# Placing each weight chunk at its own offset in its tile: a decoder layer on one core

## The chip, the cores and the metric

One Trainium2 chip, one of its cores. The metric is the device time of one execution in microseconds. The engines are TensorE (PE, its weight loads shown as PEld), VectorE (DVE), ScalarE (ACT), GpSimd (POOL) and SyncE (SP), which here only issues DMAs.

## The reference

The reference is one decoder layer on a residual stream x of 512 tokens by 1024 features in float32. An RMS norm and a projection w_in give inputs for two mixers. One is a pooling mixer with windows of 2, 4, 8 and 16 tokens, each followed by a 128 x 128 matrix. The other is a sparse attention of 8 heads with 64 features in two groups: it adds a compressed branch (blocks of 32 tokens), a selected branch and a window branch, weighted by sigmoid gates. Cut to what matters:

```
proj = rms_norm(x) @ w_in
y_pool = pooling_mixer(u) @ w_pool_out
y_nsa  = nsa_mixer(q, kv, gates) @ w_nsa_out
x = x + (gate_pool * y_pool + gate_nsa * y_nsa) @ w_out
gate_pre, val = split(rms_norm(x) @ w_up)          # 1024 -> 2 x 2816
x = x + (silu(causal_dwconv(gate_pre)) * val) @ w_down
```

With 512 tokens there are 8 blocks of 64 tokens to select from and up to 16 may be selected, so the kernel computes the selected and the window branch as full causal attention.

## The kernel before, in words

Activations are kept feature-major: 128 features on the partitions, 512 tokens along them, one such tile being a page of 2048 bytes per partition. `page()` takes them from one pool of PAGES buffers (L51).

Precision is bought with split operands. A float32 operand is cut into a high half in the matmul's number format (float32r) and a low half, which is the rest, and `mm3` (L390) issues three matmuls for each 128-row slice: high by high, high by low, low by high.

`weights()` (L373) brings a weight chunk. It takes three tiles of 1024 columns: wraw for the DMA from HBM, issued on SP; whi and wlo for the two halves. There are three buffers of each, used in turn. With lo="d" ScalarE writes -raw into wlo, a DMA issued on POOL adds raw to it in place, which leaves what the rounding of -raw had cut off, and ScalarE writes whi. Otherwise ScalarE writes whi and VectorE subtracts it from raw into wlo. The chunks come in this order of calls:

- 8 chunks of wa (768 columns) in `round_a`: queries and keys, tokens on the output partitions; here x is the stationary operand and the weights are moved, 512 and 256 columns at a time.
- 22 chunks of wf and 4 of wpo in `feature` and `pool_out`, the "feature stream", with lo="d": keys and values for the compression, pooling inputs and gates. From here on the weights are the stationary operand: 128 columns at a time are loaded, and 512 columns of activations are moved past them.
- 4 chunks of wno, 8 of wout, 44 of wup, 24 of wdn (16 with 1024 columns, 8 with 768): the dense stages that end the kernel.

A chunk of 1024 columns feeds 24 matmuls.

The order of the instructions is not the order in which the code calls them. All calls are recorded by a class `Plan`, with a price in us for each and with their dependencies; `run` (L212) then lists them, engine by engine, starting whatever can start first, and `emit` tries TRIES times with due times that come from the try before. On TensorE two streams are kept, the main one (attention and all later stages) and the feature stream, and they are mixed by the share done of each. A tile can only be given out when a buffer of its tag is free: the number of pages thus has a part in the order. wraw, whi and wlo are given out strictly in the order of calls (`FIFO`).

In the profile all of this has line L339, where the planner calls the engines; instructions are told apart by their tiles. mm, tr, av and sc are PSUM banks, xh and xl the halves of the normed input, oh and ol of the attention's output, mh and ml of the merged mixers, gh and gl of the input of the conv-MLP, yh and yl of its product, pp the attention's weights, qt and kt queries and keys.

Of the kernel before, what the change touches and what calls it, by code (L numbers as in the profile page):

```python
# [9 lines left out]
F32R = mybir.dt.float32r  # L10
# [5 lines left out]
P = 128  # L16
# [31 lines left out]
    CST[_n] = (_o, _o + _w)  # L48
    _o += _w
NCST = _o  # L50
PAGES = 54  # L51
TRIES = 8
RESERVE = 3
BASE = 5.0
# [288 lines left out]
def hybrid_layer(ctx: ExitStack, tc: tile.TileContext, xT, pos, par, cst, poolw, w1, wa, wb, wf,  # L343
                 wpo, wno, wout, wup, wdn, out):
    nc = tc.nc
    pl = Plan(nc)
    PE, ACT, DVE, POOL, SP = pl.engines
    sb = ctx.enter_context(tc.tile_pool(name="sb", bufs=1))
# [4 lines left out]
    def f32(ap):  # L353
        return ap.bitcast(F32)

    def page(name, shape=(P, T), dt=F32):
        return pl.tile(sb, shape, dt, name, "pg", PAGES)

# [6 lines left out]
    def split(dst_hi, dst_lo, src, scale=None):  # L365
# [3 lines left out]
        else:  # L369
            ACT.activation(dst_hi, src, AF.Copy, scale=scale)  # L370
            DVE.scalar_tensor_tensor(dst_lo, src, scale, f32(dst_hi), op0=ALU.mult, op1=ALU.subtract)

    def weights(ap, width, lo="d"):  # L373
        raw = pl.tile(sb, (P, 1024), F32, "wraw", "wraw", 3)
        hi = pl.tile(sb, (P, 1024), F32R, "whi", "whi", 3)
        low = pl.tile(sb, (P, 1024), F32R, "wlo", "wlo", 3)
        SP.dma_start(raw[:, :width], ap)
        if lo == "d":
            ACT.activation(low[:, :width], raw[:, :width], AF.Copy, scale=-1.0)
            POOL.dma_start(low[:, :width], raw[:, :width], accum_op=ALU.add)  # L380
            ACT.activation(hi[:, :width], raw[:, :width], AF.Copy)
        else:
            ACT.activation(hi[:, :width], raw[:, :width], AF.Copy)
            DVE.tensor_sub(low[:, :width], raw[:, :width], f32(hi[:, :width]))
        return hi, low
# [102 lines left out]
    for k in range(KD):  # L488
        if k < KD - 1:
            load_x(k + 1)  # L490
        xh[k], xl[k] = page("xh", dt=F32R), page("xl", dt=F32R)
        split(xh[k], xl[k], xr[k], mixg[:, k:k + 1])
        wak[k] = weights(wa[k], 768, "v")
        if k == 6:
            for j in range(KD):
                square_x(j)
            norm_rstd(acc, rstd, "mm")
            DVE.tensor_scalar_mul(rhalf, rstd, 0.5)
        round_a(k)
        if k == 1:  # L500
            SP.dma_start(ps_i, pos)
            SP.dma_start(cs, cst)
            SP.dma_start(pr[:, 16:], par[:, 16:])
# [47 lines left out]
    for c, (k0, k1) in enumerate(((0, 3), (3, 6), (6, 8))):  # L551
        raw = pl.tile(sb, (P, 1024), F32, "wraw", "wraw", 3)
        SP.dma_start(raw[:, :(k1 - k0) * 280], flat(wb[:, k0:k1]))
        for j in range(k1 - k0):
            home = ("pp", 10) if len(bw) < 5 else ("pt", 6)
            hi, lo = (pl.tile(sb, (P, 280), F32R, n, home[0], home[1]) for n in ("bh", "bl"))
# [88 lines left out]
    def feature(i, hi, lo):  # L645
        wh, wl = weights(flat(wf[i]), 1024)
        pt = bank("mm")
        mm3(pt, wh, wl, hi, lo, 0, KD)
        return pt
# [8 lines left out]
    with pl.on("f"):  # L658
# [50 lines left out]
        def pool_out(c):  # L709
            wh, wl = weights(wpo[c].rearrange("p a k n -> p (a k n)"), 1024)  # L710
            for f in (2 * c, 2 * c + 1):
                o = (f % 2) * 512
                pt = bank("mm")
                mm3(pt, wh[:, o:o + 512], wl[:, o:o + 512], yph, ypl, 0, 4)
                DVE.scalar_tensor_tensor(gpy[f], gpy[f], 1.0, pt, op0=ALU.add, op1=ALU.mult)
                SP.dma_start(gdr[f], gpy[f])
# [252 lines left out]
    for c in range(4):  # L969
        wh, wl = weights(wno[c].rearrange("p a k n -> p (a k n)"), 1024, "v")  # L970
        for f in (2 * c, 2 * c + 1):
# [12 lines left out]
            hi, lo = page("mh", dt=F32R), page("ml", dt=F32R)  # L984
# [11 lines left out]
    for f in range(8):  # L996
# [10 lines left out]
        hi, lo = page("gh", dt=F32R), page("gl", dt=F32R)  # L1007
# [13 lines left out]
    for f in range(KF):  # L1021
# [12 lines left out]
        if f < 8:  # L1034
            home = ("pp", 10) if f < 5 else ("pt", 6)
            hi, lo = (pl.tile(sb, (P, T), F32R, n, home[0], home[1]) for n in ("yh", "yl"))
        else:
            hi, lo = page("yh", dt=F32R), page("yl", dt=F32R)
# [112 lines left out]
```

## Time and profile before

| | |
|---|---|
| median of two runs | 717.29 us (716.8 to 717.78) |
| the profiled execution's own time | 717.68 us |
| its span, first to last instruction | 715.9 us |
| granted TensorE clock | 1.00 |
| TensorE busy | 709.5 us, 3494 instructions |
| VectorE, ScalarE, GpSimd busy | 417.7, 328.9, 31.0 us |
| moved by DMA | 90.80 MB, 127 GB/s on the mean |

In the rows of the profile "mm<-xh,whi 128\*128 128x512" is a matmul into bank mm with a stationary operand of 128 x 128 and a moving one of 128 x 512; "x176 | 73.3, 417 | 0.3" are its count, busy time in us, mean length in ns and the idle time before it. Matmuls overlap: one lasts longer than the step from its start to the start of the next, and it is the step that adds up to the span. A row of the timeline has the start in us, the length in us, the engine, the line, the operation and tiles, and a count where neighbours were merged.

### The profile page before, as it was taken

Reading aid. Unit: us, or ns where it says so; the run is one execution under the profiler, and the core shown is the slowest. Engines: PE = TensorE matmul, PEld = TensorE weight load, DVE = VectorE, ACT = ScalarE, POOL = GpSimd, SP = SyncE. Lnnn points to the kernel's source line nnn. Section 1 sums busy time; section 2 is a strip of 40 time slices with the busy share of each in tenths; the row PEclk is TensorE's granted clock in tenths of the full one; section 3 lists DMA queues with packets and bytes.
Section 4 is the critical chain, followed back from the end, with each engine's and each line's share of the span. In section 5 each row is a group of like instructions: output and inputs, shape, how many; then the busy total and the mean of one; then the engine's idle time right before and its main releaser. Section 6 shows DMA issues by size and latency. Waiting matters only on the chain.

```text
span 715.9 us, 9305 instructions
## 1 busy us (share of the span) xinstructions
PE 709.5 (99%) x3494; PEld 595.3 (83%) x3494; DVE 417.7 (58%) x874; ACT 328.9 (46%) x548; POOL 31.0 (4%) x43
## 2 busy tenths in 40 slices
PE   9999999999999999999999999999999999999997
PEld 8898888888888888888888888888888888888886
DVE  6768478878766643865576556656655663222220
ACT  8567368767677663433443343334333432121220
POOL 0001300000001000000000000000000000000000
PEclk9999999999999999999999999999999999999999
DMA  8476242654655567744322332232232333434320
GB/s 309 153 181 211 60 118 68 168 135 122 157 147 134 147 162 248 266 126 164 108 89 88 96 111 88 89 117 88 89 113 94 89 86 106 132 96 119 102 67 29
DMA packets 30573, 90.80 MB, mean 127 GB/s; under 512 B 3648, under 2 KB 3776, under 8 KB 30528
## 3 DMA queue, kind: packets, MB, share of 16 engines
q1 hardware_dynamic: 26640, 76.56, 32.5%
q0 software_dynamic: 3744, 13.63, 10.1%
q8 instruction: 27, 0.44, 0.2%
q14 instruction: 18, 0.15, 0.1%
q10 hardware_dynamic: 144, 0.01, 0.0%
HBM read 70.27 MB, written 6.29 MB: 107 GB/s over the span
## 4 chain that ended last, share of the span: by engine, by line
PE 99%; DVE 1%; issue 0%; ACT 0%; POOL 0%; ACTq 0%; POOLq 0%
PE mm L339 42%; PE tr L339 40%; PE av L339 13%; PE sc L339 3%; DVE kc L339 0%; DVE th L339 0%; DVE o L339 0%; DVE ks L339 0%; DVE qs L339 0%; ACT qs L339 0%; POOL ones L339 0%; ACTq L339 0%; ACT kt L339 0%; POOLq L1142 0%
## 5 line engine op out<-in xcount | busy, mean ns | idle before, releaser
L339 ACT ACTIVATE whi<-wraw 128x1024 fp32r<-128x1024 f32 (+1 forms) x114 | 117.2, 1028 | 213.0 <-PE tr L339 78.5
L339 DVE TENSOR_TENSOR wlo<-wraw,whi 128x1024 fp32r<-128x1024 f32 (+1 forms) x88 | 103.4, 1175 | 76.1 <-ACT whi L339 75.8
L339 PE MATMUL mm<-xh,whi 128*128 128x512 f32 x176 | 73.3, 417 | 0.3
L339 PE MATMUL mm<-xl,whi 128*128 128x512 f32 x176 | 69.0, 392 | 0.0
L339 PE MATMUL mm<-xh,wlo 128*128 128x512 f32 x176 | 69.0, 392 | 0.0
L339 PE MATMUL tr<-gh,whi 128*128 128x512 f32 x168 | 65.4, 390 | 0.0
L339 PE MATMUL tr<-gl,whi 128*128 128x512 f32 x168 | 65.4, 389 | 0.0
L339 PE MATMUL tr<-gh,wlo 128*128 128x512 f32 x168 | 65.4, 389 | 0.0
L339 PE MATMUL mm<-gh,whi 128*128 128x512 f32 x120 | 46.8, 390 | 0.0
L339 PE MATMUL mm<-gh,wlo 128*128 128x512 f32 x120 | 46.7, 389 | 0.0
L339 PE MATMUL mm<-gl,whi 128*128 128x512 f32 x120 | 46.7, 389 | 0.0
L339 PE MATMUL tr<-yh,whi 128*128 128x512 f32 x110 | 42.8, 389 | 0.0
L339 PE MATMUL tr<-yl,whi 128*128 128x512 f32 x110 | 42.8, 389 | 0.0
L339 PE MATMUL tr<-yh,wlo 128*128 128x512 f32 x110 | 42.8, 389 | 0.0
L339 PEld LDWEIGHTS mm<-xh,wlo 128*128 128x128 f32 x176 | 33.0, 188 | 7.5
L339 ACT ACTIVATE pp<-pp,asm 128x128 f32<-128x128 f32 (+3 forms) x64 | 35.3, 554 | 7.5 <-DVE asm L339 7.3
L339 PEld LDWEIGHTS mm<-xh,whi 128*128 128x128 f32 x176 | 33.2, 189 | 5.7 <-DVE th L339 1.1
L339 PEld LDWEIGHTS tr<-gl,whi 128*128 128x128 f32 x168 | 31.5, 188 | 6.5
L339 PEld LDWEIGHTS tr<-gh,whi 128*128 128x128 f32 x168 | 31.5, 188 | 6.6
L339 PEld LDWEIGHTS tr<-gh,wlo 128*128 128x128 f32 x168 | 31.5, 188 | 6.5
L339 PEld LDWEIGHTS mm<-xl,whi 128*128 128x128 f32 x176 | 33.3, 189 | 3.7
L339 ACT ACTIVATE ft<-ft 128x512 f32<-128x512 f32 x22 | 13.9, 632 | 44.1 <-DVE ft L339 44.0
(295 smaller groups left out, 1509.1 us busy)
## 6 DMA issues: line engine op xcount, KB each, us to landing
wraw<-wup SPq DMA_DIRECT2D x44, 512.0 KB, 3.3
wlo<-wraw POOLq DMA_DIRECT2D x26, 512.0 KB, 4.5
wraw<-wf SPq DMA_DIRECT2D x22, 512.0 KB, 3.4
wraw<-wdn SPq DMA_DIRECT2D x16, 512.0 KB, 3.5
wraw<-wout SPq DMA_DIRECT2D x8, 512.0 KB, 3.7
wraw<-wa SPq DMA_DIRECT2D x8, 384.0 KB, 5.2
wraw<-wdn SPq DMA_DIRECT2D x8, 384.0 KB, 3.1
xr<-xT SPq DMA_DIRECT2D x8, 256.0 KB, 6.4
```

Source lines behind the costliest of these rows:

```text
L339: getattr(self.real[o.eng], method)(*a, **kw)
```

## The change

whi and wlo become 64 columns (256 bytes) longer, and each call of `weights()` has a running number n, from 1 on. The high half of chunk n begins 4 (n mod 16) columns into its tile, which is 16n bytes modulo 256; the low half begins 4 (5n mod 16) columns into its own, 80n bytes modulo 256. All that reads or writes the halves goes by these slices. wraw stays as it is. The six tiles grow by 1536 bytes per partition together, and PAGES goes from 54 to 53, which gives up 2048.

```diff
-PAGES = 54
+PAGES = 53
...
+    shift = [0]
+
     def weights(ap, width, lo="d"):
         raw = pl.tile(sb, (P, 1024), F32, "wraw", "wraw", 3)
-        hi = pl.tile(sb, (P, 1024), F32R, "whi", "whi", 3)
-        low = pl.tile(sb, (P, 1024), F32R, "wlo", "wlo", 3)
+        n = shift[0] = shift[0] + 1
+        hi = pl.tile(sb, (P, 1088), F32R, "whi", "whi", 3)[:, n % 16 * 4:n % 16 * 4 + 1024]
+        low = pl.tile(sb, (P, 1088), F32R, "wlo", "wlo", 3)[:, n * 5 % 16 * 4:n * 5 % 16 * 4 + 1024]
         SP.dma_start(raw[:, :width], ap)
         if lo == "d":
             ACT.activation(low[:, :width], raw[:, :width], AF.Copy, scale=-1.0)
```

## The prediction

> **What bounds the kernel now.** I read the page first: the busy times, the chain and the costliest groups.
>
> ```profile
> span 715.9 us, 9305 instructions
> PE 709.5 (99%) x3494; PEld 595.3 (83%) x3494; DVE 417.7 (58%) x874; ACT 328.9 (46%) x548; POOL 31.0 (4%) x43
> ...
> PE 99%; DVE 1%; issue 0%; ACT 0%; POOL 0%; ACTq 0%; POOLq 0%
> PE mm L339 42%; PE tr L339 40%; PE av L339 13%; PE sc L339 3%; DVE kc L339 0%; DVE th L339 0%; DVE o L339 0%; DVE ks L339 0%; DVE qs L339 0%; ACT qs L339 0%; POOL ones L339 0%; ACTq L339 0%; ACT kt L339 0%; POOLq L1142 0%
> ...
> L339 ACT ACTIVATE whi<-wraw 128x1024 fp32r<-128x1024 f32 (+1 forms) x114 | 117.2, 1028 | 213.0 <-PE tr L339 78.5
> L339 DVE TENSOR_TENSOR wlo<-wraw,whi 128x1024 fp32r<-128x1024 f32 (+1 forms) x88 | 103.4, 1175 | 76.1 <-ACT whi L339 75.8
> ```
>
> TensorE is busy for 99% of the span and is 99% of the chain. The view of waits for that engine leaves it almost nothing else:
>
> ```profile
> PE mm L339 <- POOL ones L339: 1.0, 1, 1.0
> PE tr L339 <- DVE qs L339: 0.8, 1, 0.8
> PE tr L339 <- ACT qt L339: 0.2, 1, 0.2
> ```
>
> It waits 2.0 us in all. So the time is the number of matmuls times the step from one start to the next (not the 389 ns of one, since they overlap), and I went to the timeline of TensorE for that step. First the up-projection just after a few small matmuls:
>
> ```profile
> 357.39 0.40 PE L339 MATMUL mm<-gl,whi 128*128 128x512 f32 x1
> 357.62 0.40 PE L339 MATMUL mm<-gh,wlo 128*128 128x512 f32 x1
> ...
> 358.09 0.39 PE L339 MATMUL mm<-gl,whi 128*128 128x512 f32 x1
> 358.31 0.39 PE L339 MATMUL mm<-gh,wlo 128*128 128x512 f32 x1
> ...
> 359.47 0.39 PE L339 MATMUL mm<-gl,whi 128*128 128x512 f32 x1
> ...
> 359.93 0.39 PE L339 MATMUL mm<-gh,whi 128*128 128x512 f32 x1
> ...
> 362.42 0.39 PE L339 MATMUL mm<-gh,wlo 128*128 128x512 f32 x1
> ```
>
> From 357.39 to 359.47 lie nine matmuls: 2.08 / 9 = 231.1 ns each, uneven ones (358.09 to 358.31 is 0.22 us). From 359.93 to 362.42 lie eleven: 2.49 / 11 = 226.4 ns, all equal. Later it stays like that:
>
> ```profile
> 400.05 0.39 PE L339 MATMUL tr<-gh,wlo 128*128 128x512 f32 x1
> 400.27 0.39 PE L339 MATMUL tr<-gh,whi 128*128 128x512 f32 x1
> ...
> 401.86 0.39 PE L339 MATMUL tr<-gl,whi 128*128 128x512 f32 x1
> ```
>
> Eight steps in 1.81 us are 226.3 ns; I use 226.5. The stream thus has a settled step of 226.5 ns and an unsettled one of 231.1 ns, and needs about nine matmuls after a disturbance to settle. In the stage where attention and feature chunks alternate it seldom settles:
>
> ```profile
> 214.77 1.11 PE L339 MATMUL sc<-kt,qt 128*128 128x256 f32 x8
> 215.72 0.40 PE L339 MATMUL mm<-xh,whi 128*128 128x512 f32 x1
> 215.95 0.40 PE L339 MATMUL mm<-xl,whi 128*128 128x512 f32 x1
> 216.19 0.39 PE L339 MATMUL mm<-xh,wlo 128*128 128x512 f32 x1
> ...
> 217.11 0.60 PE L339 MATMUL tr<-cs,pp 128*128 128x128 f32 x4
> ```
>
> Six matmuls from 215.72 to 217.11 take 1.39 us, 231.7 ns each, and the longest step, 215.95 to 216.19, is 0.24 us. Eight 256-wide ones before them take 0.95 us, 119 ns each.
>
> **The change, part by part.** *The number of instructions.* None is added or removed: the 3434 matmuls of the program, its copies and its DMAs are the same. What changes is the address from which each weight load reads, the address to which ScalarE, VectorE and the accumulating DMA write, and, through the page count, the planner's order.
>
> *The weight loads.* In the dense stages the weights are the stationary operand: 4 chunks of wno, 8 of wout, 44 of wup and 24 shorter ones of wdn give 96 + 192 + 1056 + 528 = 1872 matmuls of 512 columns, and the 26 chunks of the feature stream 624 more, 2496 in all. Every large tile of the built kernel starts at 128 modulo 256 bytes and each 128-column slice is 512 bytes long, so every weight load and every moving read starts at the same place modulo 256. No row shows another placement; the price has to be bounded. That steps of one shape and one granted clock come out at 226.5 or 231.1 ns, by what ran just before, tells me that the reads are sensitive to their phase. A weight load lies beside the matmul ahead of it:
>
> ```profile
> L339 PEld LDWEIGHTS tr<-gh,whi 128*128 128x128 f32 x168 | 31.5, 188 | 6.6
> L339 PEld LDWEIGHTS tr<-gl,whi 128*128 128x128 f32 x168 | 31.5, 188 | 6.5
> ```
>
> At 188 ns it fits in the 226.5 ns, with 38 ns to spare, so a load that only lengthened by a few ns would cost nothing. What can cost is the step itself. Lower end of the usual kind: every chunk settles at once, 0 us. Upper end: none settles, 1872 x (231.1 - 226.5) = 1872 x 4.6 ns = 8.6 us. My value goes by the nearest row, the nine unsettled matmuls after a disturbance: each chunk now starts at another offset than the one before it, so I count nine unsettled matmuls in each of the 1872 / 24 = 78 full chunks' worth: 78 x 9 x 4.6 ns = 3.2 us. In chunks with an odd n the two halves lie 64 or 192 bytes apart, modulo 256, and the stream goes back and forth between them; that this keeps them unsettled is possible, and it is what the upper end holds. The feature stream is unsettled already (231.7 ns), so it gets nothing.
>
> *Weights as the moving operand.* In the first stage xh is stationary and whi, wlo are moved, 8 chunks x 24 matmuls 512 wide = 192. Bounded by the same 4.6 ns either way, +-0.9 us. I take 0.
>
> *ScalarE and VectorE.* The splits write and read at shifted places. A slower one is covered as long as these engines have room in the dense stage:
>
> ```profile
> 400.00:450.00 50.00, 50.00 (x222) 41.38 (x222) 29.14 (x36) 18.80 (x23) 0.00 (x0) 1.00 0.32 105
> ```
>
> Columns: TensorE, weight loads, VectorE 29.14 and ScalarE 18.80 us of 50, at a granted clock of 1.00. A chunk lasts 24 x 226.5 = 5.4 us, VectorE needs 3.2 of it, so its 1175 ns subtraction could grow by 2.2 us before it is late. I take 0, bounds 0 to 0.
>
> *The accumulating DMA.* Its destination is no longer at the same place modulo 256 for each chunk. From the view of tile wlo in the feature stage:
>
> ```profile
> L339 PE MATMUL mm<-xh,wlo x176: 387/392/417, 54.6 to 285.3; 128*128 128x512 f32 x176
> L339 POOL DMA_DIRECT2D wlo<-wraw x25: 859/862/934, 38.0 to 269.5; - x25
> ...
> DMA to landing us min/median/max: 4.5/4.5/7.2
> ```
>
> The last one is issued at 269.5 and lands at 274.0; the last matmul on its chunk starts at 285.3 and the first seven triples earlier, 7 x 0.69 = 4.9 us, so at 280.4. The least slack is 6.4 us, and the transfer may last 2.4 times as long before TensorE waits. Behind it on the POOL queue stand only the other accumulates. I take 0; what it would be without the cover is a rival.
>
> *One page fewer.* The order on TensorE moves between about the fifth and the eleventh chunk of the feature stream and is nearly the same afterwards; on SP one load of a feature chunk moves past a store of a gate and two reloads of tn swap places with gp; on POOL one accumulate moves behind two additions of kcb. TensorE can win no more than its 2.0 us of waits; a missing page could hold one chunk back, 5.4 us at most if nothing else were ready. Nearest is the present state, hardly any wait: 0, bounds -2.0 and +5.4.
>
> *Sum.* The profiled execution took 717.68 us (span 715.9 and 1.8 around it), 0.4 above the median of 717.29. 717.7 + 3.2 = 720.9, on the median 720.5.
>
> A rule of the Trainium skill speaks against this term: TensorE: Matmul & The Clock Gate, Part 2, step 1, says that TensorE reads weights and the moving operand by two independent ports, so that loading the next weights takes no bandwidth from the running matmul. By that rule the term is 0 and the sum 717.3 on the median; the trace's two steps for one shape do not fit it, but no run here varies the address.
>
> **The rivals.** *No influence of the address (not slower, not faster).* The steps differ by the mix of instructions alone and the weight loads read beside it all. For it: 38 ns of spare time after each load. Against it: 231.1 ns within one chunk, with nothing but 512-wide matmuls, settling only after nine. It gives 717.3, plus the order's -2 to +5.
>
> *Faster: the reads stop colliding.* Two 256-wide steps make 238 ns and one 512-wide 226.5; a straight line through 119 and 226.5 ns has a slope of 107.5 ns per 256 columns and 11.5 ns that do not grow with the width. If that part is a collision of weight load and moving read at equal addresses and spreading ends it, 2496 x 11.5 = 28.7 us go: 688.6. Over 2%, 14.3 us, needs 5.7 ns of it, a mean step of 220.8. Against it: no step in the quoted rows is under 0.22 us even where phases vary, and the spread goes through all offsets, so good and bad ones mix. The middle, 703, is what I would expect of it. The same page of the Trainium skill, Back-to-back issue gap, has 512 / 2.4 + 2.5 = 215.8 ns; by that figure an estimate of the most to be won is 2496 x 10.7 = 26.7 us.
>
> *Slower by over 2%: a worse beat that holds.* Halves at different offsets keep the whole dense part at the longest step seen, 0.24 us by rounded starts, so at least 235 ns: 1872 x 8.5 = 15.9 us, and 624 x (235 - 231.7) = 2.1 us in the feature stream: 735.3. It decides from a dense step of 234.1 on (14.3 / 1872 = 7.6 ns). For it: such steps occur singly. Against it: they have always been mixed with short ones.
>
> *Slower: the accumulate or a page.* The quoted row has 25 accumulates from 38.0 to 269.5, one in 9.6 us. If a transfer took three times as long, 13.5 us, each would come 3.9 us later than the one before it, and 24 x 3.9 less the slack of 6.4 is 87 us. Against it: it needs a threefold transfer. A page held back costs the 5.4 us above.
>
> **How the numbers follow.** The likeliest case, unsettled starts of chunks, has 0.30 and gives 720.5, with its own range of 717 to 726. No influence has 0.22, at 717.3. Both are within 2%: 0.52. A worse beat has 0.24, transfers and pages 0.07: slower by over 2%, 0.31. Collisions that end have 0.17. Two per cent is about what a measurement of this kernel can tell from no change. The range takes in half of the faster case and the worse beat with some of the order's loss: 702 to 740; some 0.12 lies below it and 0.07 above.
>
> **What would show it.** In the profile after: the step between 512-wide matmuls in the dense stage, chunk by chunk, since n is known for each. Nine uneven steps of about 231 ns at a chunk's start and 226.5 after them would show the term right; 226.5 throughout, no influence; steps under 0.22, the faster rival; 235 and more, the slower. Whether odd n differ from even n tells if the distance between halves matters. The landing of wlo<-wraw near 4.5 us, and TensorE waits near 2 us, would show the other terms at 0. I am wrong if TensorE is no longer 99% of the chain.

## The result, and the profile after

The changed kernel takes 728.01 us in the median of two runs (727.65 to 728.37) against 717.29: a ratio of 1.0149, 95% interval 1.0106 to 1.0193. It is 1.5% slower: less than the 2% from which the prediction counts a change, though the interval leaves no doubt of the sign. The profiled execution took 727.65 us, 9.97 more than that of before, and its span is 10.0 us longer.

From the page of the changed kernel, the span, the busy times, the chain and three of the groups:

```profile
span 725.9 us, 9304 instructions
PE 719.8 (99%) x3494; PEld 595.4 (82%) x3494; DVE 419.6 (58%) x874; ACT 328.3 (45%) x548; POOL 30.5 (4%) x43
...
PE 98%; DVE 1%; DMA 0%; ACT 0%; issue 0%
...
L339 DVE TENSOR_TENSOR wlo<-wraw,whi 128x1024 fp32r<-128x1024 f32 (+1 forms) x88 | 103.4, 1175 | 77.2 <-ACT whi L339 77.2
...
L339 PE MATMUL tr<-gh,whi 128*128 128x512 f32 x168 | 66.3, 395 | 0.0
...
L339 PEld LDWEIGHTS tr<-gh,whi 128*128 128x128 f32 x168 | 31.6, 188 | 7.2
```

TensorE has as many records and is busy for 10.3 us longer; of the other engines none changes by more than 2 us. A weight load still lasts 188 ns, VectorE's subtraction still 1175 ns. Only the matmul is longer, 395 ns where it was 389 to 390.

TensorE makes up 98% of the chain and not 99%, which the prediction named as a sign of being wrong. By lines it is 98.1% after 98.5%, and what came in is 0.4% of the first weight loads (DMA wraw<-wa), so the bound is still TensorE. Its waits in the changed kernel add up to 1.9 us, against 2.0:

```profile
PE mm L339 <- POOL ones L339: 1.0, 1, 1.0
PE mm L339 <- DVE kc L339: 0.6, 1, 0.6
PE tr L339 <- ACT xh L339: 0.3, 1, 0.3
```

Where the time comes from is shown by the first and the last matmuls of the dense stages, from the views of the tiles oh and yh. The two times after the lengths are the first and the last start in us. Before:

```profile
L339 PE MATMUL tr<-oh,whi x20: 389/389/389, 285.5 to 306.6; 128*128 128x512 f32 x20
L339 PE MATMUL tr<-yh,wlo x110: 388/389/389, 592.5 to 711.5; 128*128 128x512 f32 x110
```

After:

```profile
L339 PE MATMUL tr<-oh,whi x20: 390/397/398, 285.7 to 307.3; 128*128 128x512 f32 x20
L339 PE MATMUL tr<-yh,wlo x110: 387/394/399, 599.8 to 721.4; 128*128 128x512 f32 x110
```

Up to the dense part the two kernels differ by 0.2 us (285.5 and 285.7). The dense part takes 711.5 - 285.5 = 426.0 us before and 721.4 - 285.7 = 435.7 after: 9.7 of the 10.0 us. The mean step there, worked out from all starts in the trace except four longer steps across the small matmuls of the norm, rose from 226.70 to 231.94 ns, and 1872 x 5.24 ns = 9.8 us.

The timeline of TensorE shows how, since n is known for each chunk. These are the edges of the chunks 63, 64 and 65 of the changed kernel; each bank's 24 matmuls are one chunk:

```profile
443.46 0.39 PE L339 MATMUL mm<-gh,whi 128*128 128x512 f32 x1
...
448.99 0.39 PE L339 MATMUL tr<-gh,whi 128*128 128x512 f32 x1
...
454.43 0.39 PE L339 MATMUL av<-gh,whi 128*128 128x512 f32 x1
454.66 0.40 PE L339 MATMUL av<-gl,whi 128*128 128x512 f32 x1
...
456.99 0.39 PE L339 MATMUL av<-gh,wlo 128*128 128x512 f32 x1
```

Chunk 64, with both halves at 0, takes 5.44 us for 24 steps: 226.7 ns, settled from its first matmul. Chunk 63 (240 and 176 bytes) takes 5.53 us, 230.4 ns. In chunk 65 (16 and 80 bytes) the ten steps from 454.66 on take 2.33 us, 233 ns. What follows the first nine steps of a chunk is no shorter than the whole: 231.82 ns in the mean over the 16 values of n mod 16, against 231.94. So most chunks are not unsettled for a while and then settled; each value of n mod 16 has a mean step that comes back, within about 0.5 ns, each time the value does (chunks 48 and 49, next to the norm's small matmuls, excepted) and holds to the end of the chunk. Odd and even n do not differ: 231.9 ns each.

The accumulating DMA shows nothing; its landing in the feature stream of the changed kernel:

```profile
L339 POOL DMA_DIRECT2D wlo<-wraw x25: 859/859/899, 37.5 to 269.3; - x25
...
DMA to landing us min/median/max: 4.5/4.5/7.3
```

### The profile page after: what moved, and what is told of

The parts are those of the page before. It is cut to its first block, busy times and chain, and to the rows that moved or that the text cites. A ratio compares the mean times of both kernels' runs of the same rounds, so it can differ in the third digit from the quotient of the medians.

```text
span 725.9 us, 9304 instructions
## 1 busy us (share of the span) xinstructions
PE 719.8 (99%) x3494; PEld 595.4 (82%) x3494; DVE 419.6 (58%) x874; ACT 328.3 (45%) x548; POOL 30.5 (4%) x43
## 4 chain that ended last, share of the span: by engine, by line
PE 98%; DVE 1%; DMA 0%; ACT 0%; issue 0%
PE mm L339 41%; PE tr L339 40%; PE av L339 13%; PE sc L339 3%; DMA wraw<-wa 0%; DVE th L339 0%; DVE kc L339 0%; ACT xh L339 0%; DVE o L339 0%; DVE ks L339 0%; ACT whi L339 0%; ACT kt L339 0%; ACT ks L339 0%
## 5 line engine op out<-in xcount | busy, mean ns | idle before, releaser
L339 DVE TENSOR_TENSOR wlo<-wraw,whi 128x1024 fp32r<-128x1024 f32 (+1 forms) x88 | 103.4, 1175 | 77.2 <-ACT whi L339 77.2
L339 ACT ACTIVATE wlo<-wraw 128x1024 fp32r<-128x1024 f32 x26 | 27.5, 1059 | 15.5 <-PE mm L339 12.8
```

The costliest lines, as they stand in the source:

```text
L339: getattr(self.real[o.eng], method)(*a, **kw)
```

## The experiments

The theory (A in the texts below): the step between matmuls depends on where the weight load starts, modulo 256, relative to the moving operand, and lastingly so. Its rivals: (B) the planner's order with one page fewer costs the time; (C) only the changing of places unsettles the stream; (A2) the weights' own place counts, whatever the moving operand's is; and that ScalarE, VectorE or the DMAs bring the cost in. Runs 1, 2 and 12 are medians of 10, 4 and 10 executions, the others are one execution each. Executions of one kernel differ by up to 1.5 us (run 1: 716.35 to 717.81), so the argument goes by the dense step, worked out from the trace as above.

**1. Pages and tile length without the shift.** Edit to the changed kernel:

```diff
-        hi = pl.tile(sb, (P, 1088), F32R, "whi", "whi", 3)[:, n % 16 * 4:n % 16 * 4 + 1024]
+        hi = pl.tile(sb, (P, 1088), F32R, "whi", "whi", 3)[:, 0:0 + 1024]
...
+        low = pl.tile(sb, (P, 1088), F32R, "wlo", "wlo", 3)[:, 0:0 + 1024]
```

> Tiles of 1088 columns and 53 pages as in the changed kernel, with the planner's order of it, but every half at offset 0. Theory A (the place of the weights relative to the moving operand sets the step): the dense step is 226.7 ns again, the time 717 to 718 us. Theory B (the order with one page fewer costs the time): about 728 us, with the dense step still at 226.7 ns, since that stage has no choice of order.

Measured: 717.38 us, ratio to the kernel before 0.9992, interval 0.9982 to 1.0001; dense step 226.70 ns. Theory B falls: with the instructions in the same order as in the changed kernel the whole loss is gone.

**2. Both halves at 64 bytes, always.** As 1, with 16 in place of 0 in both lines.

> Both halves of every chunk at 64 bytes. Theory A: the chunks with both halves at 64 bytes stepped at 233.3 ns in the changed kernel, so the whole dense part does: 1872 x (233.3 - 226.7) = 12.4 us over the kernel without shift, about 730 us. Theory C (only changes from chunk to chunk and from half to half unsettle the stream, any constant place settles): 226.7 ns and 717 to 718 us.

Measured: 731.18 us, ratio 1.0185, interval 1.0168 to 1.0202; dense step 233.34 ns from the first chunk to the last. Theory C falls: nothing changes from chunk to chunk here and the stream never settles at 226.7. Its timeline has a beat of two:

```profile
400.63 0.40 PE L339 MATMUL tr<-gh,whi 128*128 128x512 f32 x1
400.86 0.39 PE L339 MATMUL tr<-gl,whi 128*128 128x512 f32 x1
401.09 0.40 PE L339 MATMUL tr<-gh,wlo 128*128 128x512 f32 x1
401.33 0.39 PE L339 MATMUL tr<-gh,whi 128*128 128x512 f32 x1
...
404.83 0.40 PE L339 MATMUL tr<-gh,whi 128*128 128x512 f32 x1
```

From 400.63 to 404.83 lie 18 matmuls in 4.20 us: 233.3 ns each, longer and shorter by turns.

**3 and 4. One offset for both halves, in lines of 16 bytes and in single columns.** As the changed kernel, with `n % 16 * 4` in both lines, and with `n % 16` in both.

> Both halves at 16n bytes modulo 256, so the two halves never differ. Theory A: a step for each of the 16 places, 226.7 ns at 0, 233.3 at 64 and 128, 229.3 at 192, others between 226.7 and 235; time 726 to 730 us. Theory C: each chunk unsettled for its first nine matmuls and 226.7 after that: 721 us.

Measured: 726.84 us; mean dense step 231.64 ns. With both halves at the same place the loss is nearly that of the change, so the distance between the halves is not what matters most. At 0 and 240 bytes, and in four of the five chunks at 16 bytes, the stream steps at 226.7 for most of a chunk, elsewhere at 229.2 (192 bytes) to 234.3 (96 bytes).

> Both halves at 4n bytes modulo 64, so single columns. Theory A says that the step depends on the place; if a line of 16 bytes is what counts, the four places within a line give one step, and 0 to 12 bytes give 226.7 ns; 16, 32 and 48 bytes give what the run with 16n shows. A step below 226.7 anywhere would make a faster kernel. Theory C: 721 us, alike for all places.

Measured: 728.32 us; mean 232.15 ns. The guess about lines of 16 bytes was wrong: at 4, 8 and 12 bytes the step is 232.3, 230.9 and 230.0 (last fifteen steps of a chunk), within 16 bytes of the place that gives 226.7.

The two runs also show that the place alone does not always fix the step. A chunk at 16 bytes follows one at 0 bytes in run 3 and one at 12 bytes in run 4. Here is one of each, from its first matmul to the first of the next chunk. Run 3:

```profile
454.19 0.39 PE L339 MATMUL av<-gh,whi 128*128 128x512 f32 x1
...
459.64 0.39 PE L339 MATMUL mm<-gh,whi 128*128 128x512 f32 x1
```

Run 4:

```profile
471.56 0.39 PE L339 MATMUL tr<-gh,whi 128*128 128x512 f32 x1
...
477.16 0.39 PE L339 MATMUL mm<-gh,whi 128*128 128x512 f32 x1
```

The 24 steps take 5.45 and 5.60 us: 227 and 233 ns at the same place. In run 3 itself, the first chunk at 16 bytes starts just after the norm's small matmuls and keeps 233.3 ns to its end, while the four later ones have 227.0. So at some places the stream can hold more than one step, and what ran before decides between them. Theory A does not say this, and theory C has that much in its favour.

**5 and 6. Moving the pages.** 5 is kernel 1 with a tile of 64 bytes allotted ahead of the pages, 6 is 5 with both halves at 192 bytes.

```diff
     ones = keep("ones", (P, P))
+    pad = keep("pad", (P, 16))
+    POOL.memset(pad, 0.0)
```

> No shift within the weight tiles, but 64 bytes of padding ahead of the pages, so that pages and weights both lie at 192 modulo 256 instead of 128. If the place relative to the moving operand counts (theory A): 226.7 ns and 717 to 718 us. If the weights' own place modulo 256 counts (A2): 233.3 ns as with both halves at 64 bytes, about 731 us.

Measured: 716.98 us; dense step 226.71 ns.

> The same padding, and both halves at 192 bytes in their tiles: the weights lie at 128 modulo 256 as in the kernel before, the pages at 192. Theory A: the place of the weights relative to the pages is 192, which stepped at 229.2 ns in the changed kernel: 1872 x 2.5 = 4.7 us, about 722 us. A2: 226.7 ns and 717 to 718 us.

Measured: 720.74 us; dense step 228.90 ns. Here the weights lie exactly where they lie, modulo 256, in the kernel before, and the step is that of 192 bytes. Both runs say that the place relative to the pages counts, and A2 falls. From 6:

```profile
400.02 0.39 PE L339 MATMUL tr<-gh,wlo 128*128 128x512 f32 x1
...
402.31 0.39 PE L339 MATMUL tr<-gh,whi 128*128 128x512 f32 x1
```

Ten steps in 2.29 us: 229 ns.

**7. Only wraw shifted.** Kernel 1 with wraw 1088 columns long and its data 64 bytes in, and 52 pages (which changes the planner's order once more).

> Only wraw is shifted, by 64 bytes, and the halves stay at 0 (52 pages, to make room): the DMA writes and ScalarE, VectorE and the accumulating DMA read at another place than before, TensorE does not. Theory A: 226.7 ns and 717 to 719 us. If the placement hurts by way of the other engines' accesses, the dense step rises as with the halves at 64 bytes, towards 731 us.

Measured: 718.15 us; dense step 226.70 ns. The accesses of the DMA, ScalarE and VectorE at the shifted place cost nothing that shows in the step.

**8. The stream by itself.** The layer is left out; sections of 96 matmuls run on fixed tiles, between two short ones, with nothing else at work:

```python
for i in range(count):
    a, b = (i // 3 % 8) * P + w(i) % 64, (i % 8) * 512 + m(i) % 64
    nc.tensor.matmul(pt[0:cols, 0:n], W[:, a:a + cols], M[:, b:b + n], start=True, stop=True)
```

> None of the layer is computed: only sections of 96 matmuls each on fixed tiles, and no other engine at work. Theory A: with weights 0, 16, 64, 128 and 192 bytes past the moving operand's place the steps are 226.7, 226.7, 233.3, 233.3 and 229.2 ns as in the layer, so that TensorE's two reads alone make them; both moved together by 64 or 192 bytes give 226.7. With a moving operand that starts 16, 32, 48, 64 or 128 bytes further on for each matmul the step may fall below 226.7, to 216 if a full round of lines is what the settled step waits for (224 to 236 otherwise). Loads of 32, 64 and 96 columns: 218, 221 and 224 ns if each line of a load costs the same, 226.7 if loads cost nothing at this place. Widths of 256, 384, 448, 480, 496: 120, 173, 200, 213 and 227 ns if the step goes in units of 13.33 ns; 113, 170, 198, 213 and 220 if it goes with the width.

Steps after the first thirty of a section, from the starts in the trace (the sections with the weights at 0, 16 and 32 bytes run together in the records; their joint stretch steps at 226.7 ns for its first two thirds and at 233.3 for the last):

| weights, moving operand at (bytes) | step, ns |
|---|---|
| 64, 0 / 128, 0 / 192, 0 | 233.4 / 232.3 / 228.9 |
| 64, 64 / 192, 192 | 226.7 / 226.7 |
| 0, 64 / 0, 192 | 228.9 / 233.3 |
| 0, further on by 16, 32, 48, 64, 128, 224, 240 each time | 230.5, 234.2, 231.6, 231.7, 230.1, 231.7, 235.0 |
| both further on by 16, 32, 64 each time | 230.4, 232.5, 228.3 |
| 0, 0 with 32, 64, 96 columns loaded | 231.6, 229.9, 230.0 |
| 0, 0 with 256, 384, 448, 480, 496 columns moved | 120.0, 173.3, 206.7, 216.7, 223.3 |

The layer's steps at 64, 128 and 192 bytes come back to within about 1 ns without any other engine, so TensorE's two reads are enough to make them. Moving operand at 64 with the weights at 0 is as good as weights at 192 with the moving operand at 0, as theory A has it. The rest of the guesses went wrong: a moving operand that walks on is never below 226.7; loads of fewer columns don't shorten the step, they lengthen it by 3 to 5 ns. Widths of 256 and 384 columns, and 512 of the settled layer, step at 120.0, 173.3 and 226.7: 53.3 ns for each 128 columns, and 13.3 ns that do not grow with them. The widths of 448, 480 and 496 lie 3 to 7 ns above that line.

**9. All 64 places.** As 8, sections of 48, the weights 0 to 252 bytes past the moving operand's place. The steps are those after the first twenty of a section.

> None of the layer is computed: 64 sections of 48 matmuls of 512 columns, with the weights 0, 4, 8 ... 252 bytes past the place of the moving operand, nothing else at work. Theory A: 226.7 ns at 0, the values of the layer at 64, 128 and 192 bytes (233.3, 233.3 and 229.0), and nothing below 226.7, so that the placement of the kernel before is already the best. If the collision of equal places were what the fixed 13.3 ns are (the faster rival), some places would step at 216 to 220.

Nothing steps below 226.67 ns. That value comes at 0, 16, 28, 120, 132 and 156 bytes; 31 places lie within 0.4 ns of 233.3, the others from 228.3 (240 bytes) to 238.0 (164 bytes). The expected 233.3, 233.3 and 229.0 at 64, 128 and 192 bytes were 233.3, 232.4 and 228.9. Most places that runs 3 and 4 also had agree with them within 1 ns; 12, 28 and 240 bytes, as well as 16, do not (233.3, 226.7 and 228.3 here; 230.0 and 234.9 in run 4 and 226.7 in run 3). The table is thus that of this order of places, each entered after the short matmuls between sections. The timeline merges each section into one row; here are the sections at 0, 4, 8, 12 and 16 bytes:

```profile
20.77 11.15 PE L372 MATMUL pt<-m,w 128*128 128x512 f32 x48
...
32.23 11.39 PE L372 MATMUL pt<-m,w 128*128 128x512 f32 x48
...
43.94 11.32 PE L372 MATMUL pt<-m,w 128*128 128x512 f32 x48
...
55.57 11.44 PE L372 MATMUL pt<-m,w 128*128 128x512 f32 x48
...
67.33 11.13 PE L372 MATMUL pt<-m,w 128*128 128x512 f32 x48
```

The second column is the section's length: 11.15 and 11.13 us at 0 and 16 bytes, 11.32 to 11.44 between.

**10 and 11. One half alone at 64 bytes.** Kernel 1 with 16 in place of 0 in the line of hi, or in that of low.

> High halves at 64 bytes, low halves at 0, in all chunks. If each load costs what its own place costs, two of three loads are at 64 bytes: (2 x 233.3 + 226.7) / 3 = 231.1 ns and 1872 x 4.4 = 8.3 us more than without shift, 725.5 us. If the halves only have to agree with each other, or if the going back and forth has a cost of its own, the step is that of both at 64, 233.3 ns, or above, 730 us and more.

Measured: 730.38 us; dense step 233.32 ns.

> Low halves at 64 bytes, high halves at 0. Each load by its own place: (233.3 + 2 x 226.7) / 3 = 228.9 ns and 4.1 us more, 721.5 us. A cost of going back and forth: the same as with only the high halves shifted, 230 ns or more.

Measured: 725.30 us; dense step 231.11 ns. The loads' costs don't add up place by place: 231.1 and 228.9 had been expected for the two. The triple high, high, low has a beat of its own, and one displaced load of three already costs 4.4 ns a step.

**12. Both halves at 120 bytes.** As 2, with 30 in place of 16.

> Both halves of every chunk at 120 bytes, one of the six places that stepped at 226.67 ns in the bare stream. If that table of places holds for the layer too: 226.7 ns and 717 to 718 us, the same as without shift. If in the layer every place but 0 unsettles the stream: 230 to 233 ns, 724 to 730 us.

Measured: 716.73 us, ratio 0.9984, interval 0.9974 to 0.9993; dense step 226.69 ns. The settled step at 120 bytes comes back in the layer: a shift as such does no harm. The dense part begins a little earlier than with no shift (first the view of tile oh of run 1, then of run 12):

```profile
L339 PE MATMUL tr<-oh,whi x20: 389/389/389, 285.0 to 306.1; 128*128 128x512 f32 x20
```

```profile
L339 PE MATMUL tr<-oh,whi x20: 389/389/389, 284.5 to 305.5; 128*128 128x512 f32 x20
```

That is 0.5 us, in the stage where attention and feature stream are mixed. The trace accounts for most of it: neighbouring 512-wide matmuls of the feature stream step at 229.2 ns in the mean, against 230.1 in run 1, which over 438 such steps is 0.4 us. In the time it is not clear of the noise: run 1 already measures 0.08% below the kernel before, run 12 0.16%, and their intervals overlap.

## Why the prediction was right and where it was wrong

*The place of the step.* Right. The bound is the step between TensorE's matmuls, and the dense part gave 9.7 of the 10.0 us of span. That the mean step of 231.94 ns is close to the 231.1 ns of the rows from 357.39 to 359.47 is chance: the one is a mean over chunks of 226.7 to 233.5 ns, the other a stream on its way to 226.7. The measured 728.01 lies in the range of 702 to 740, but above the 717 to 726 of the likeliest case: it was the room left for a worse beat that took it in.

*The term of the weight loads.* The sign was right, the size and the way were not. The step that failed is "each chunk now starts at another offset than the one before it, so I count nine unsettled matmuls": 78 x 9 x 4.6 ns = 3.2 us, where 9.8 were measured. It took the settled step for something that the stream comes back to by itself at any offset. Run 2 shows that it doesn't: at 64 bytes throughout, 233.34 ns never settles. Run 1 and chunk 64 show where the settling came from: the two reads started at the same place (run 12: or at another of the few distances that settle). Only there does the picture of the prediction hold: in run 4 the chunks at 0 bytes settle after some five uneven steps. The upper end, 8.6 us for a stream that never settles, was closer, and still too low: it took 231.1 ns for the unsettled step, and many places hold 233.

*The feature stream.* The prediction gave it nothing, since it was unsettled already. It is not at its longest, though: neighbouring 512-wide matmuls there step at 230.1 ns in run 1, 231.8 in the changed kernel and 233.4 in run 2, all with the same order, and the dense part begins at 285.0, 285.7 and 286.8 us. So in these executions the change cost some 0.7 us there, most of it hidden by the new order, which without the shift begins the dense part 0.5 us earlier (285.5 before, 285.0 in run 1). The 231.7 ns of the prediction came from six matmuls.

*The distance between the halves.* The prediction gave the odd n a part in it, and passed over n = 2, 6, 10 and 14 modulo 16, where the halves lie 128 bytes apart. Odd and even n have the same mean, and run 3, with no distance at all, has 231.64 against 231.94, so little hangs on it. But the halves are not independent either (runs 10 and 11).

*The order and the pages.* Taken as 0 within -2.0 to +5.4; run 1 measures -0.08% with an interval of -0.18 to +0.01%. Right.

*Two smaller readings.* The matmuls that the prediction counts as 3434 are 3494 in the page; nothing hangs on it. The prediction takes 2% for about the least that can be told from no change. The two executions of each kernel lie within 0.14% of each other and the interval is 0.4% to either side, so the measured 1.5% is clear.

*ScalarE, VectorE, the accumulate.* Taken as 0. The subtraction stayed at 1175 ns and the landing at 4.5 us. Right.

*The rule on two ports.* The page TensorE: Matmul & The Clock Gate, Part 2, of the Trainium skill says that loading the next tile's weights takes no SBUF read bandwidth from the running matmul; by that rule the term would be 0. Runs 1, 2 and 8 do not fit that for these float32r streams: moving only the place of the load costs 6.6 ns a matmul. Whether the two reads share a port, or something behind it, or delay each other in another way is not shown.

*The faster rival.* It put the 13.3 ns (by rounded rows 11.5) that do not grow with the width down to a collision at equal places. Run 9 refutes it: equal places are among the best six of 64, and none is below. What these 13.3 ns are stays open, and so does why just these six places settle. Only the relation is shown, not a mechanism in the memory.

*The slower rivals.* A worse beat that holds is what came, at 231.9 and not at 235 ns; by the prediction's sum a dense step of 234.1 was needed for 2%. The slow accumulate did not happen.

## What to carry to other kernels

Where TensorE is the bound, read the step from start to start in the timeline, not the length of a matmul: two streams of one shape and one clock can differ by 3% (226.7 and 233.3 ns). A step that is equal throughout is not yet the best one: with both operands 16 bytes further on each time, run 8 steps at an even 230.4 ns. In a dense float32r stream, keep the weights and the moving operand at the same place modulo 256 bytes, as they were in the kernel before, and read the step again after any change of a tile's length or of what is allotted before it. A drifting offset is not a safe middle: most places cost, and none that was tried makes the dense step shorter.

## What the runs showed of the hardware that had not been expected

- A matmul of 512 columns with its own load of 128 steps at 226.67 ns at best, and 4 bytes decide: 226.67 at 0 and 16, 232.2 at 4 bytes (run 9).
- The same place can hold two steps, by what ran before: at 16 bytes 227.0 ns after a chunk at 0 bytes (run 3), 233.4 after one at 12 bytes (run 4).
- The relation is between the two operands. 64 bytes on both gives 226.7, the moving operand at 64 alone 228.9, the weights at 64 alone 233.4 (run 8).
- Fewer columns in the load do not help: 32, 64 and 96 columns step at 231.6, 229.9 and 230.0 ns where 128 step at 226.7 (runs 8 and 9).
- The step for 256, 384 and 512 columns is 120.0, 173.3 and 226.7 ns, so a fixed 13.3 ns for each matmul with its load (runs 8 and 9).
